# All products with the high weight parts before all with the low parts, within each output tile

## The chip, the cores and the metric

The kernel runs on one core of a Trainium2 chip. TensorE (PE) multiplies; ScalarE (ACT) and VectorE (DVE) prepare its operands and read its results; GpSimd (POOL) does some of the elementwise work; SyncE (SP) issues the loads of the weights. The metric is the device time of one execution in microseconds (us). Before the change it is 2869.92 us, the median of three runs (2869.36 to 2870.63).

## The reference, cut to what matters

The program is a two-layer trunk over 256 tokens with 2048 features. Each layer has a mixer, a cross attention to 256 memory tokens and a gated MLP of width 5632, each behind an RMS norm and each added to the running state `h`. The mixer of layer 0 is a short convolution beside a diagonal state-space scan ("S5"), that of layer 1 a sliding-window attention.

```python
def conv_ssm_mixer(h, w_in, ...):
    z = h @ w_in
    gate_b, gate_c, xa, u = jnp.split(z, [A_WIDTH, 2 * A_WIDTH, 3 * A_WIDTH], axis=-1)
    ya = gate_b * causal_dwconv(gate_c * xa, conv_w)
    ys = s5_branch(u, ...)
    return jnp.concatenate([ya, ys], axis=-1) @ w_out

def conv_gated_mlp(h, w_gate, w_up, conv_w, conv_b, w_down):
    g = causal_dwconv(h @ w_gate, conv_w) + conv_b
    return (jax.nn.silu(g) * (h @ w_up)) @ w_down
```

All of this is float32. Nearly all the arithmetic lies in the dense projections, `h @ w` with 128-feature blocks of both sides.

## The kernel before, in words

**Split operands.** Every weight block and every activation block is split into two parts, high and low, each in the reduced float32 format that TensorE takes (`fp32r`). Of the four products three are summed: high weight x high activation, high weight x low activation, low weight x high activation. An activation block is one tile `op`, 128x512: the high parts of 256 tokens, then the low parts of the same tokens.

**Output tiles.** A projection is computed in tiles of 128 output features (n-tiles), each a sum over K blocks of 128 input features (k-tiles; K is 16, or 11 in the MLP's down projection). `gemm` walks over the n-tiles. For each, `wload` has SP load one raw weight block, then ACT casts a chunk of 1024 columns (8 k-tiles) to its high part (`hi`, L90) and DVE subtracts to get the low part (`lo`, L91). A tile of 16 k-tiles has two chunks, which are called chunk 0 and chunk 1 here. The pools hold three raw blocks, four `hi` chunks and four `lo` chunks, so two n-tiles' worth of each: a chunk of n-tile i+2 is written into the place of the same chunk of n-tile i, once TensorE has read that for the last time.

**The matmuls.** `mm` takes the k-tiles in order. For each it issues one matmul of 512 columns with `hi` (L106, both activation parts, into the two halves of a PSUM bank) and one of 256 columns with `lo` (L107, into the first half), so that the two widths alternate. With `one` set (memory keys, gates, the very last tile) the 512-column matmul is replaced by two of 256 columns with the same `hi` (L103, L104). Each matmul loads its own 128x128 weights (PEld in the profile). The memory values (L326 to L328) and the attention values (L681 to L683) have the weights as the streamed operand and three matmuls per k-tile.

**Order of the work.** A scheduler orders the instructions of each engine when the program is built, by its own estimates; each engine then works through its list in order. So an ACT or DVE instruction that waits holds up all that stand behind it on its engine. TensorE's order is nearly that in which the code issues the matmuls.

**The stages.** Up to about 560 us the profile shows the even mixer: the first projection tiles (up to about 50 us), the memory keys (L103, L104, L107) and values (L326 to L328) of both layers, and the gates (from about 460 us, again L103, L104 and L107). Beside these DVE and ACT work through the S5 scan (L493 on ACT, L497 to L500 on DVE). The scan is handed out in portions, one behind each n-tile (`after`). Then follow the output projection, cross attention 0 (from about 720 us), MLP 0 (926 to 1653 us), the odd mixer (to about 1900 us), cross attention 1, and MLP 1 (2108 to 2837 us). In the odd mixer and in cross attention `half` puts a piece of the attention into the middle of an n-tile (in the odd mixer the transposes L745 of a head pair) and `after` puts other pieces behind it (the scores L713 and L716, then the values L759).

## Time and profile before

| what | value |
|---|---|
| median of three runs | 2869.92 us |
| span of the profiled execution | 2856.4 us |
| what the runs have beyond that span | 13.5 us |
| TensorE matmuls, busy | 2813.3 us, 98% of the span |
| VectorE busy | 1942.5 us, 68% |
| ScalarE busy | 1560.2 us, 55% |
| HBM read | 521.25 MB, 186 GB/s over the span |

The profile gives for the profiled execution its span, from the first to the last instruction; no other time of that execution is given. A busy share of TensorE counts overlapping matmuls as busy, so the pace of the matmuls is read from the start of one to the start of the next.

### The profile page before, as it was taken

Reading aid. Unit: us, or ns where it says so; the run is one execution under the profiler, and the core shown is the slowest. Engines: PE = TensorE matmul, PEld = TensorE weight load, DVE = VectorE, ACT = ScalarE, POOL = GpSimd, SP = SyncE. Lnnn points to the kernel's source line nnn. Section 1 sums busy time; section 2 is a strip of 40 time slices with the busy share of each in tenths; the row PEclk is TensorE's granted clock in tenths of the full one; section 3 lists DMA queues with packets and bytes.
Section 4 is the critical chain, followed back from the end, with each engine's and each line's share of the span. In section 5 each row is a group of like instructions: output and inputs, shape, how many; then the busy total and the mean of one; then the engine's idle time right before and its main releaser. Section 6 shows DMA issues by size and latency. Waiting matters only on the chain.

```text
span 2856.4 us, 44117 instructions
## 1 busy us (share of the span) xinstructions
PE 2813.3 (98%) x17163; PEld 2473.4 (87%) x17163; DVE 1942.5 (68%) x3130; ACT 1560.2 (55%) x2556; POOL 496.5 (17%) x484
## 2 busy tenths in 40 slices
PE   9999999999999999999999999999999999999998
PEld 8878978998988888888888888889888888888887
DVE  8978688757667666666666778776766566665655
ACT  7666766655554544545545567555555454454454
POOL 4100201322002320202202210110122022021121
PEclk9999999999999999999999999999999999999999
DMA  7455554545555556555455554464455554554544
GB/s 276 175 201 187 200 199 177 196 177 192 192 184 181 192 172 211 187 176 201 171 209 187 182 190 169 152 217 171 170 191 185 170 205 164 205 190 163 207 169 141
DMA packets 91811, 534.65 MB, mean 187 GB/s; under 512 B 10865, under 2 KB 17361, under 8 KB 40913
## 3 DMA queue, kind: packets, MB, share of 16 engines
q1 hardware_dynamic: 86368, 522.56, 51.8%
q10 hardware_dynamic: 5232, 9.26, 0.9%
q8 instruction: 134, 2.20, 0.3%
q14 instruction: 77, 0.62, 0.1%
HBM read 521.25 MB, written 10.53 MB: 186 GB/s over the span
## 4 chain that ended last, share of the span: by engine, by line
PE 90%; DVE 6%; ACT 3%; issue 1%; DMA 0%; POOL 0%; SPq 0%; DVEq 0%; ACTq 0%; POOLq 0%
PE ps L106 49%; PE ps L107 27%; PE ps L103 3%; PE ps L104 3%; DVE lo L91 2%; ACT stmp L493 2%; PE ps L327 1%; PE ps L326 1%; PE ps L328 1%; DVE stmp L497 1%; DVE S L498 1%; ACT hi L90 1%; PE m L850 1%; PE m L759 0%; DVE S L499 0%
## 5 line engine op out<-in xcount | busy, mean ns | idle before, releaser
L106 PE MATMUL ps<-op,hi 128*128 128x512 f32 x6069 | 2133.0, 397 | 0.7 <-DVE op L75 0.7
L107 PE MATMUL ps<-op,lo 128*128 128x256 f32 x6976 | 1956.3, 280 | 14.8 <-DVE lo L91 14.5
L91 DVE TENSOR_TENSOR lo<-raw,hi 128x1024 fp32r<-128x1024 f32 (+2 forms) x1033 | 1185.7, 1150 | 710.1 <-ACT hi L90 697.1
L90 ACT CAST hi<-raw 128x1024 fp32r<-128x1024 f32 (+2 forms) x1033 | 1009.9, 982 | 989.6 <-PE ps L106 822.6
L106 PEld LDWEIGHTS ps<-op,hi 128*128 128x128 f32 x6069 | 1138.9, 188 | 273.7 <-issue 3.0
L107 PEld LDWEIGHTS ps<-op,lo 128*128 128x128 f32 x6976 | 1319.1, 189 | 20.1 <-DVE lo L91 19.4
L103 PE MATMUL ps<-op,hi 128*128 128x256 f32 x907 | 259.1, 286 | 3.2 <-ACT hi L90 3.2
L104 PE MATMUL ps<-op,hi 128*128 128x256 f32 x907 | 257.7, 284 | 0.0
L167 POOL TENSOR_TENSOR acc<-acc,t 128x256 f32<-128x256 f32 x112 | 124.1, 1108 | 633.8 <-ACT t L169 627.3
L887 POOL TENSOR_TENSOR t<-t,rbc 128x256 f32<-128x256 f32 x88 | 71.4, 811 | 783.5 <-DVE t L156 752.2
L103 PEld LDWEIGHTS ps<-op,hi 128*128 128x128 f32 x907 | 175.0, 193 | 5.2 <-ACT hi L90 3.5
L104 PEld LDWEIGHTS ps<-op,hi 128*128 128x128 f32 x907 | 175.0, 193 | 0.1
L893 POOL TENSOR_TENSOR t<-t,rbc 128x256 f32<-128x256 f32 x88 | 124.2, 1411 | 289.2 <-ACT t L892 289.2
L493 ACT ACTIVATE stmp<-S,s_pw 128x256 f32<-128x256 f32 (+3 forms) x256 | 115.5, 526 | 41.2 <-DVE S L500 34.8
L327 PE MATMUL ps<-lo,op 128*128 128x512 f32 x256 | 101.6, 397 | 6.2 <-DVE lo L91 6.0
L326 PE MATMUL ps<-hi,op 128*128 128x512 f32 x256 | 101.3, 396 | 1.0 <-ACT hi L90 1.0
L328 PE MATMUL ps<-hi,op 128*128 128x512 f32 x256 | 100.5, 393 | 0.0
L156 DVE TENSOR_TENSOR t<-ps,t 128x256 f32<-128x256 f32 x232 | 96.5, 417 | 0.0
L68 DVE SCALAR_TENSOR_TENSOR op<-h,gains,op 128x256 fp32r<-128x256 f32 x96 | 83.6, 880 | 12.5 <-ACT op L67 12.5
L155 ACT COPY t<-ps 128x256 f32<-128x256 f32 x232 | 83.4, 361 | 3.0 <-PE ps L107 2.2
L305 POOL TENSOR_TENSOR kst<-t,rbc 128x256 f32<-128x256 f32 x32 | 32.7, 1022 | 261.3 <-DMA kv<-kst 131.6
L280 DVE TENSOR_TENSOR h<-h,ps 128x256 f32<-128x256 f32 x95 | 39.6, 419 | 50.9 <-PE ps L107 50.6
(218 smaller groups left out, 1858.9 us busy)
## 6 DMA issues: line engine op xcount, KB each, us to landing
raw<-in_ff_gate SPq DMA_DIRECT2D x88, 1024.0 KB, 4.8
raw<-in_ff_up SPq DMA_DIRECT2D x88, 1024.0 KB, 4.8
raw<-in_ff_down SPq DMA_DIRECT2D x128, 704.0 KB, 4.1
raw<-in_xa_k SPq DMA_DIRECT2D x32, 1024.0 KB, 4.9
raw<-in_xa_v SPq DMA_DIRECT2D x32, 1024.0 KB, 4.9
raw<-in_xa_q SPq DMA_DIRECT2D x32, 1024.0 KB, 4.8
raw<-in_xa_o SPq DMA_DIRECT2D x32, 1024.0 KB, 4.8
raw<-in_ev_w_in SPq DMA_DIRECT2D x28, 1024.0 KB, 4.9
```

The costliest lines, as they stand in the source:

```text
L90: nc.scalar.copy(hi, s)
L91: nc.vector.tensor_tensor(lo, s, hi.bitcast(F32), op=ALU.subtract)
L103: nc.tensor.matmul(ps[:, :T], lhsT=hi, rhs=o[:, :T], start=k == 0, stop=False)
L104: nc.tensor.matmul(ps[:, :T], lhsT=hi, rhs=o[:, T:], start=False, stop=False)
L106: nc.tensor.matmul(ps, lhsT=hi, rhs=o, start=k == 0, stop=False)
L107: nc.tensor.matmul(ps[:, :T], lhsT=lo, rhs=o[:, :T], start=False, stop=k == K - 1)
L167: nc.gpsimd.tensor_tensor(self.acc, self.acc, self.sq, op=ALU.add)
L326: nc.tensor.matmul(ps[b], lhsT=xh, rhs=hi, start=k == 0, stop=False)
L327: nc.tensor.matmul(ps[b], lhsT=xh, rhs=lo, start=False, stop=False)
L328: nc.tensor.matmul(ps[b], lhsT=xl, rhs=hi, start=False, stop=k == KT - 1)
L493: nc.scalar.activation(tmp[:, x, :, p - p0, :], at(0, both, p), AF.Copy, scale=pw[:, x, k, 8 * b + p:8 * b + p + 1])
L893: nc.gpsimd.tensor_tensor(y, y, self.rbc, op=ALU.mult)
```

## The change

Within each n-tile the matmuls with `hi` of all k-tiles now come first, then those with `lo` of all k-tiles. `mm` is divided into `mm_hi` and `mm_lo`. `half` is called between the two phases, where it was called after half of the k-tiles. The first four n-tiles of the input projection do the same within each loaded step of 1 to 4 k-tiles, and the memory values and the attention values within each loaded weight block. The number and shape of all instructions stay as they were. The rest of the diff takes comments away and moves lines.

```diff
-    def mm(self, ps, w, ops, k0, k1, K, one=False):
+    def mm_hi(self, ps, w, ops, k0, k1, one=False):
         nc = self.nc
         for k in range(k0, k1):
-            hi, lo = w[k]
-            o = ops[k]
+            hi, o = w[k][0], ops[k]
             if one:
                 nc.tensor.matmul(ps[:, :T], lhsT=hi, rhs=o[:, :T], start=k == 0, stop=False)
                 nc.tensor.matmul(ps[:, :T], lhsT=hi, rhs=o[:, T:], start=False, stop=False)
             else:
                 nc.tensor.matmul(ps, lhsT=hi, rhs=o, start=k == 0, stop=False)
-            nc.tensor.matmul(ps[:, :T], lhsT=lo, rhs=o[:, :T], start=False, stop=k == K - 1)
+
+    def mm_lo(self, ps, w, ops, k0, k1, K):
+
+        for k in range(k0, k1):
+            self.nc.tensor.matmul(ps[:, :T], lhsT=w[k][1], rhs=ops[k][:, :T], start=False, stop=k == K - 1)
+
+    def mm(self, ps, w, ops, k0, k1, K, one=False, half=None):
+
+        self.mm_hi(ps, w, ops, k0, k1, one)
+        if half is not None:
+            half()
+        self.mm_lo(ps, w, ops, k0, k1, K)
...
-            if half is None:
-                self.mm(ps, w, ops, 0, k1, K, one(n) if callable(one) else one)
-            else:
-                self.mm(ps, w, ops, 0, K // 2, K, one)
-                half(n)
-                self.mm(ps, w, ops, K // 2, k1, K, one)
+            self.mm(ps, w, ops, 0, k1, K, one(n) if callable(one) else one, half=None if half is None else lambda: half(n))
...
-                        nc.tensor.matmul(ps[b], lhsT=xh, rhs=hi, start=k == 0, stop=False)
-                        nc.tensor.matmul(ps[b], lhsT=xh, rhs=lo, start=False, stop=False)
-                        nc.tensor.matmul(ps[b], lhsT=xl, rhs=hi, start=False, stop=k == KT - 1)
+                        nc.tensor.matmul(ps[b], lhsT=o[:, b * P:(b + 1) * P], rhs=w[j][0], start=k == 0, stop=False)
+                        nc.tensor.matmul(ps[b], lhsT=o[:, T + b * P:T + (b + 1) * P], rhs=w[j][0], start=False, stop=False)
+                for j in range(4):
+                    k = 4 * q + j
+                    for b in range(2):
+                        nc.tensor.matmul(ps[b], lhsT=self.memop[k][:, b * P:(b + 1) * P], rhs=w[j][1], start=False, stop=k == KT - 1)
```

Two places show what the scheduler makes of it. The first is TensorE in the odd mixer, inside the n-tile whose sum is `ps_18707` (K is 16; `hi_18699` and `lo_18700` are its chunk 0, `hi_18703` and `lo_18704` its chunk 1, `s_18600` or `s_18597` the weights of a head pair that are transposed). Before:

```order
L107 MATMUL ps_18707<-op_17933,lo_18700 128x256
L106 MATMUL ps_18707<-op_18035,hi_18699 128x512
L107 MATMUL ps_18707<-op_18035,lo_18700 128x256
L745 MATMUL m_18724<-ident_91,s_18600 128x128 x3
L745 MATMUL m_18730<-ident_91,s_18600 128x128 x3
L106 MATMUL ps_18707<-op_18137,hi_18703 128x512
L107 MATMUL ps_18707<-op_18137,lo_18704 128x256
L106 MATMUL ps_18707<-op_18239,hi_18703 128x512
L107 MATMUL ps_18707<-op_18239,lo_18704 128x256
L106 MATMUL ps_18707<-op_18341,hi_18703 128x512
```

And now:

```order
L105 MATMUL ps_18707<-op_18341,hi_18703 128x512
L105 MATMUL ps_18707<-op_18443,hi_18703 128x512
L105 MATMUL ps_18707<-op_18545,hi_18703 128x512
L751 MATMUL m_18721<-ident_91,s_18597 128x128 x3
L751 MATMUL m_18727<-ident_91,s_18597 128x128 x3
L110 MATMUL ps_18707<-op_17321,lo_18700 128x256
L110 MATMUL ps_18707<-op_17423,lo_18700 128x256
L110 MATMUL ps_18707<-op_17525,lo_18700 128x256
```

The transposes stood between the 8th and the 9th k-tile, with matmuls of both widths on either side. Now all 16 wide matmuls are in front of them and all 16 narrow ones behind.

The second is DVE in the memory keys of layer 0, where it makes the low parts for the n-tile with raw block `raw_1707` among steps of the scan (`S_966` is the state, `stmp` its temporaries). Before:

```order
L498 TENSOR_TENSOR S_966<-S_966,stmp_2193 128x512
L91 TENSOR_TENSOR lo_1710<-raw_1707,hi_1709 128x1024
L499 TENSOR_TENSOR S_966<-S_966,stmp_2193 128x256
L500 TENSOR_TENSOR S_966<-S_966,stmp_2193 128x256
L497 TENSOR_TENSOR stmp_2315<-S_966,s5_pw_1391 128x256 x2
L498 TENSOR_TENSOR S_966<-S_966,stmp_2315 128x256
L91 TENSOR_TENSOR lo_1714<-raw_1707,hi_1713 128x1024
L499 TENSOR_TENSOR S_966<-S_966,stmp_2315 128x128
L500 TENSOR_TENSOR S_966<-S_966,stmp_2315 128x128
L497 TENSOR_TENSOR stmp_2387<-S_966,s5_pw_1391 128x128 x2
```

And now:

```order
L502 TENSOR_TENSOR stmp_2193<-S_966,s5_pw_1391 128x512 x2
L503 TENSOR_TENSOR S_966<-S_966,stmp_2193 128x512
L504 TENSOR_TENSOR S_966<-S_966,stmp_2193 128x256
L91 TENSOR_TENSOR lo_1710<-raw_1707,hi_1709 128x1024
L91 TENSOR_TENSOR lo_1714<-raw_1707,hi_1713 128x1024
L505 TENSOR_TENSOR S_966<-S_966,stmp_2193 128x256
L502 TENSOR_TENSOR stmp_2315<-S_966,s5_pw_1391 128x256 x2
L503 TENSOR_TENSOR S_966<-S_966,stmp_2315 128x256
L504 TENSOR_TENSOR S_966<-S_966,stmp_2315 128x128
```

The scan steps that stood between the low parts of chunk 0 and chunk 1 have moved out of that gap: the two low parts of an n-tile now stand next to each other.

The third is DVE in the odd mixer, between one head pair (`s_17388`, with its softmax numbers `st_17399`) and the next (`s_17490`, which reads the scores in `m_17491`). Before:

```order
L732 TENSOR_TENSOR st_17399<-st_17399 128x4
L733 RECIPROCAL st_17399<-st_17399 128x4
L736 TENSOR_SCALAR s_17388<-s_17388,st_17399 128x256
L736 TENSOR_SCALAR s_17388<-s_17388,st_17399 128x128
L736 TENSOR_SCALAR s_17388<-s_17388,st_17399 128x256
L736 TENSOR_SCALAR s_17388<-s_17388,st_17399 128x128
L91 TENSOR_TENSOR lo_17637<-raw_17630,hi_17636 128x1024
L156 TENSOR_TENSOR t_17481<-ps_17436,t_17482 128x256
L718 SCALAR_TENSOR_TENSOR s_17490<-m_17491,bias_17488 128x256
L719 SCALAR_TENSOR_TENSOR s_17490<-m_17491,bias_17488 128x128
```

And now:

```order
L91 TENSOR_TENSOR lo_17633<-raw_17630,hi_17632 128x1024
L91 TENSOR_TENSOR lo_17637<-raw_17630,hi_17636 128x1024
L738 TENSOR_TENSOR st_17399<-st_17399 128x4
L161 TENSOR_TENSOR t_17481<-ps_17436,t_17482 128x256
L739 RECIPROCAL st_17399<-st_17399 128x4
L724 SCALAR_TENSOR_TENSOR s_17490<-m_17491,bias_17488 128x256
L742 TENSOR_SCALAR s_17388<-s_17388,st_17399 128x256
L742 TENSOR_SCALAR s_17388<-s_17388,st_17399 128x128
L742 TENSOR_SCALAR s_17388<-s_17388,st_17399 128x256
L742 TENSOR_SCALAR s_17388<-s_17388,st_17399 128x128
L725 SCALAR_TENSOR_TENSOR s_17490<-m_17491,bias_17488 128x128
```

Before, the low part of chunk 0 of the n-tile with raw block `raw_17630` stood ahead of the reciprocal (it is not among these rows), that of chunk 1 between the scaling of one head pair and the reading of the next scores. Now both stand ahead of the reciprocal, and the scaling follows the first reading of the next scores.

## Rows read from the trace of the kernel before

**Rows 1.** The page: the span, and of the chain of work that ended last the shares by engine.

```profile
span 2856.4 us, 44117 instructions
...
PE 90%; DVE 6%; ACT 3%; issue 1%; DMA 0%; POOL 0%; SPq 0%; DVEq 0%; ACTq 0%; POOLq 0%
```

**Rows 2.** What TensorE waited for, by stretch: first 0 to 35 us (two rows), then 110 to 166, 166 to 355 (two rows), 355 to 400 (two rows) and 475 to 530 us (two rows). Columns: engine, tile and line that waited, what released it; us in total, times, longest us.

```profile
PE ps L254 <- DVE lo L91: 2.1, 4, 0.9
PE ps L253 <- ACT hi L90: 1.8, 2, 1.5
...
PE ps L107 <- DVE lo L91: 9.3, 10, 1.7
...
PE ps L327 <- DVE lo L91: 1.9, 3, 1.1
PE ps L107 <- DVE lo L91: 0.7, 2, 0.5
...
PE ps L327 <- DVE lo L91: 4.2, 6, 1.4
PE ps L326 <- ACT hi L90: 1.0, 1, 1.0
...
PE ps L107 <- DVE lo L91: 4.2, 4, 1.3
PE ps L103 <- ACT hi L90: 3.2, 1, 3.2
```

**Rows 3.** Stretches of the trace, of the 512-column matmuls L106 alone: start and end, length, PE busy (x matmuls), PEld busy (x loads), granted clock, DMA share, GB/s. In each stretch the widths alternate, so the count is one of pairs.

```profile
626.00:706.00 80.00, 80.00 (x227) 42.54 (x227) 1.00 0.52 186
926.00:1653.00 727.00, 726.80 (x2097) 392.85 (x2097) 1.00 0.55 190
1670.00:1900.00 230.00, 193.38 (x537) 100.73 (x537) 1.00 0.48 168
2108.00:2837.00 729.00, 728.80 (x2063) 387.46 (x2063) 1.00 0.52 183
```

**Rows 4.** The timeline of TensorE where matmuls of one width follow each other: start us, us, line, shapes. Between the first two rows lie 35 further matmuls of 256 columns (so 36 steps), between the next two 18 of 512 columns (19 steps), between the last two 11 of 256 columns (12 steps), each with its own weight load.

```profile
99.75 0.28 PE L103 MATMUL ps<-op,hi 128*128 128x256 f32 x1
...
104.07 0.28 PE L103 MATMUL ps<-op,hi 128*128 128x256 f32 x1
...
420.00 0.39 PE L327 MATMUL ps<-lo,op 128*128 128x512 f32 x1
...
424.31 0.39 PE L328 MATMUL ps<-hi,op 128*128 128x512 f32 x1
...
2840.06 0.28 PE L107 MATMUL ps<-op,lo 128*128 128x256 f32 x1
...
2841.50 0.29 PE L107 MATMUL ps<-op,lo 128*128 128x256 f32 x1
```

**Rows 5.** The same timeline behind a stop of TensorE in the memory values, all of 512 columns: 9 steps from the first row to the second, 4 from the second to the third.

```profile
425.87 0.39 PE L327 MATMUL ps<-lo,op 128*128 128x512 f32 x1
...
427.95 0.39 PE L327 MATMUL ps<-lo,op 128*128 128x512 f32 x1
...
428.86 0.39 PE L328 MATMUL ps<-hi,op 128*128 128x512 f32 x1
```

**Rows 6.** Stretches with all engines: start and end, length, busy us (x instructions) of PE, PEld, DVE, ACT, POOL, then granted clock, DMA share, GB/s.

```profile
116.00:155.00 39.00, 30.50 (x237) 28.68 (x237) 36.95 (x71) 16.05 (x26) 3.72 (x5) 1.00 0.43 156
...
355.00:400.00 45.00, 39.65 (x193) 30.00 (x193) 41.22 (x84) 23.56 (x39) 3.13 (x2) 0.96 0.44 160
...
460.00:520.00 60.00, 52.48 (x426) 49.69 (x426) 53.95 (x95) 32.86 (x59) 12.22 (x11) 0.97 0.48 171
```

**Rows 7.** The timeline of TensorE at a wait for a low part (the first two rows), at the wait for a high part (the next two), and from there on: 24 steps lie between the last two rows. In brackets the idle time before and what ended it.

```profile
122.74 0.28 PE L104 MATMUL ps<-op,hi 128*128 128x256 f32 x1
124.76 0.39 PE L107 MATMUL ps<-op,lo 128*128 128x256 f32 x1 [1.74 <-DVE lo L91]
...
512.81 0.28 PE L107 MATMUL ps<-op,lo 128*128 128x256 f32 x1
516.25 0.39 PE L103 MATMUL ps<-op,hi 128*128 128x256 f32 x1 [3.16 <-ACT hi L90]
...
517.88 0.41 PE L103 MATMUL ps<-op,hi 128*128 128x256 f32 x1
...
523.00 0.41 PE L103 MATMUL ps<-op,hi 128*128 128x256 f32 x1
```

**Rows 8.** A short stretch of TensorE right behind that wait: start and end, length, PE busy (x), granted clock, DMA share, GB/s.

```profile
517.00:520.00 3.00, 2.49 (x11) 0.50 0.29 116
```

**Rows 9.** The timeline of ACT before that wait: a step of the scan and the cast for which TensorE waited.

```profile
504.34 3.02 ACT L493 ACTIVATE stmp<-S,s_pw 128x126 f32<-128x126 f32 x7 [9.83 <-DVE S L500]
...
515.15 1.04 ACT L90 CAST hi<-raw 128x1024 fp32r<-128x1024 f32 x1
```

**Rows 10.** The timeline of one n-tile's end in the odd mixer: DVE makes a low part, ACT copies a head pair's transposed weights (`pT`), TensorE runs scores (L713) and values (L759).

```profile
1734.13 1.22 DVE L91 TENSOR_TENSOR lo<-raw,hi 128x1024 fp32r<-128x1024 f32 x1
1736.09 0.83 ACT L748 COPY pT<-m 128x384 f32<-128x384 f32 x2
1736.25 0.70 PE L713 MATMUL m<-kT,q 64*128 64x256 f32 x4
1737.10 0.88 PE L759 MATMUL m<-pT,vt 128*64 128x128 f32 x12
```

More of the change, by code (lines that the diff above doesn't have):

```diff
@@ L138, in gemm @@
         for n, w, ps in held:
-            self.mm(ps, w, ops, K - late, K, K, one)
+            self.mm(ps, w, ops, K - late, K, K, one(n) if callable(one) else one)
             if mid2 is None:
@@ L677, in odd_mixer @@
                     k = 8 * q + j
[L678 removed]
                     for b in range(2):
[L680 to L683 removed]
+                        nc.tensor.matmul(pv[b][:, :T], lhsT=xs[k][:, b * P:(b + 1) * P], rhs=w[j][0], start=k == 0, stop=False)
+                        nc.tensor.matmul(pv[b][:, :T], lhsT=xs[k][:, T + b * P:T + (b + 1) * P], rhs=w[j][0], start=False, stop=False)
+                for j in range(8):
+                    k = 8 * q + j
+                    for b in range(2):
+                        nc.tensor.matmul(pv[b][:, :T], lhsT=xs[k][:, b * P:(b + 1) * P], rhs=w[j][1], start=False, stop=k == KT - 1)
                 if q == 0:
```

24 lines of the change are left out of this document (8 added, 16 removed).

## The prediction

> **What bounds the kernel now.** The page comes first: the chain of work that ended last is 90% TensorE in a span of 2856.4 us [rows 1]. So TensorE's list of matmuls is the path, and only two things can change the time: the pace at which matmuls follow each other, and the time TensorE stands still. The number and shape of the matmuls stay as they are.
>
> The second view is what TensorE waited for, by stretch [rows 2]. Behind the start-up it waits only up to 530 us, beside the S5 scan, for DVE's low parts (9.3 + 1.9 + 0.7 + 4.2 + 4.2 = 20.3 us in 25 waits) and for ACT's high parts (1.0 + 3.2 = 4.2 us in 2). DVE is nearly full there: 36.95 of 39 us, 41.22 of 45, 53.95 of 60 [rows 6].
>
> The third view is the pace, from starts of matmuls. Where the widths alternate, a pair (512 then 256 columns) takes 727.00 / 2097 = 0.3467 us in MLP 0, but 729.00 / 2063 = 0.3534 us in MLP 1, and 80.00 / 227 = 0.3524 us in the even mixer's output projection, all at granted clock 1.00 with TensorE busy throughout [rows 3]. The same pair has two paces, 6.7 ns apart, and nothing that waits explains it. The fourth view is runs of one width: 256 columns take (104.07 - 99.75) / 36 = 0.1200 us, and again (2841.50 - 2840.06) / 12 = 0.1200 us in the very last tile, right behind the slow MLP 1; 512 columns take (424.31 - 420.00) / 19 = 0.2268 us [rows 4]. A pair made of such steps costs 0.2268 + 0.1200 = 0.3468 us, the faster of the two paces.
>
> **The change part by part.**
>
> *Pace.* Inside a phase every matmul now follows one of its own width. I price a pair at 0.3468 us everywhere. MLP 1 gains 2063 x (0.3534 - 0.3468) = 13.6 us; the output projection of the even mixer, 16 n-tiles of 16 pairs, 256 x (0.3524 - 0.3468) = 1.4 us; the odd mixer, with 537 pairs [rows 3], 537 x 0.0066 = 3.5 us if they run at MLP 1's pace. That last pace is an assumption, since its row mixes in the attention's small matmuls. MLP 0 loses 2097 x 0.0001 = 0.2 us. Sum: 18 us less. The two changes of width per n-tile I price at nothing, because alternation is nothing but changes of width and its faster pace equals the sum of the pure ones. What no row shows is 512 columns directly behind 256 with no stop, followed by more 512. The nearest row is the memory values behind a stop: nine steps at (427.95 - 425.87) / 9 = 0.2311 us before they settle at 0.2275 [rows 5]. By it each n-tile would pay 9 x (0.2311 - 0.2268) = 0.04 us; over 422 n-tiles with wide matmuls (counted from the code) that is 16 us. I take zero, and keep -18 and -2 as the ends.
>
> The Trainium skill ("TensorE: Matmul & The Clock Gate", section "Back-to-back issue gap") gives the isolated gap between matmuls as set by the column count alone, about N/2.4 + 2.5 ns when the clock is up. By that rule a pair is an estimated 325 ns in any order, and reordering is worth nothing. The trace disagrees with both halves: the pair takes 0.3467 us or 0.3534 us, not one value. That order has no effect on the pace is a rival below, priced from rows.
>
> *Low parts are wanted later.* In the memory keys and gates an n-tile is 48 steps of 0.12 us, 5.76 us. Before, `lo` of chunk 0 was wanted at the third matmul (0.24 us in) and `lo` of chunk 1 at 3.1 us; now at 32 x 0.12 = 3.84 us and 4.80 us. DVE's order has the two low parts side by side, that of chunk 0 behind about the same scan steps as before, that of chunk 1 behind fewer. So a DVE that runs late may be 3.6 us later before TensorE notices. That is a stock that is spent once in each stretch where DVE is the slower engine, not a gain per tile: DVE's work is unchanged and it has only 2 of 39 us free. Keys, 110 to 166 us: 3.6 of 9.3 us. From 166 to 355 us: five separate waits, none over 1.1 us, all inside the stock: 2.6 us, and 5 x 0.16 us for starting again (124.76 - 122.74, less 1.74 idle and one step of 0.12 [rows 7]), 3.4 us. Memory values, 355 to 400 us: a block's low parts are wanted 16 wide steps later instead of one, 15 x 0.2268 = 3.4 us of the 4.2 + 0.2. Gates, 475 to 530 us: 3.6 of 4.2 us. Sum: 14 us less. The ends are 0 (the scheduler has moved scan work in front and eats the stock) and all 20.3 + 4.2 us of waits with 27 x 0.16 us of restarts and the clock loss behind the longest, 24 steps at (523.00 - 517.88) / 24 = 0.2133 instead of 0.12 us, 2.2 us, at a granted clock of 0.50 [rows 7, 8]: 31 us.
>
> *High parts.* `hi` of chunk 0 is wanted at the start of its tile, as before, and that of chunk 1 a third into it instead of half: 0.96 us earlier in the keys and gates. Each `hi` buffer also comes free earlier, a third and two thirds into its last tile instead of half and the end. Outside the scan TensorE waits for no cast at all, so I price this at 0 there. Inside the scan ACT may stand behind a scan step that waits for DVE, as it did for 9.83 us before the cast that ended at 516.19 [rows 9]. I leave that wait of 3.2 us where it is. DVE's wait for a free `lo` buffer moves from half a tile to five sixths; what stands behind it on DVE (scan steps, evacuations) has four PSUM banks of slack.
>
> *`half` between the phases.* In the odd mixer the transposes now stand 16 x 0.12 = 1.9 us before the tile's end instead of 8 x 0.3534 = 2.8 us. ACT's copy of their result is the margin: it ends at 1736.92 and the values start at 1737.10, 0.18 us later, behind the scores at 1736.25 [rows 10]. The copy started over 2 us after its transposes because the softmax stands before it on ACT, and DVE's low part of 1.22 us is one of the things that softmax competes with. Pairing the low parts can bring that chain forward or push it by one low part. The ends: 0, and 13 tiles x (1.22 - 0.18) = 13.5 us. I take 0: both low parts now stand ahead of the reciprocal on DVE, where the second can start when its buffer comes free at the tile's end, so they are about done when the next scores come, and none is left between the scaling and the reading of those scores.
>
> *Start and end.* The first 35 us have 3.9 us of waits [rows 2]; phases of up to 16 wide matmuls tolerate a late low part but want four operands at once. I take 0, with 2 us either way. Behind the last matmul nothing changes.
>
> **Sum.** -18 - 14 = -32 us on the profiled span of 2856.4 us, which gives 2824 us. The runs have 13.5 us beyond that span, which no instruction of the change touches: 2869.9 - 32 = 2838 us.
>
> **The rivals.**
>
> *A. Order does not set the pace*: the 6.7 ns of MLP 1 come from something that outlasts the reorder, such as the addresses of the operands. For it: that pace holds evenly over 729 us. Against it: the last tile runs at 0.1200 us right behind. The 18 us are gone: 2856 us.
>
> *B. Wide matmuls settle anew in each tile* [rows 5]. The 16 us come back: 2854 us. Against it: rows 5 follow a stop, and the phases follow none.
>
> *C. The stock is eaten*: DVE is full beside the scan, and its waits return at their old length. 2852 us.
>
> *D. Slower.* The casts become the bound beside the scan. A third instead of half a tile takes 0.96 us from every cast of chunk 1; in ACT's list it stands behind scan steps that wait for DVE [rows 9]. If it is late in each of the 27 places where TensorE waits today, that is 26 us; the old waits stay, and the odd mixer loses its 13.5 us: 2870 - 18 + 26 + 13 = 2891 us, or 2878 us without the odd mixer. It decides where casts end less than 0.96 us before use. Against it: ACT is half idle there, 16.05 of 39 us busy [rows 6].
>
> **How the numbers follow.** The forecast has 0.56, with a range of its own of 2824 to 2850 us; A 0.13, B 0.11, C 0.12, D 0.08. About 0.2% (5.7 us, so 2864 to 2876 us) is what a measurement of this kernel can tell from no change. The forecast, C and nearly all of A and B are faster: 0.85; two rivals that meet, as A with C, come to 2870 us, and I give 0.08 to no change; slower has D's remainder, 0.07. The range is 2822 us (all the pace and nearly twice the stock) to 2864 us (A with most of C).
>
> **What would show it.** Pace right: 512-column steps of 0.227 us and 256-column steps of 0.120 us in both MLPs, and MLP 1 as long as MLP 0. A: MLP 1 stays at 0.353 us per pair. B: the first nine wide steps of each tile near 0.231 us. Stock right: waits for low parts up to 530 us fall from 20 us to about 8 us. C: they keep their sum. D: waits for ACT's casts grow from 4 us to tens of us, or TensorE waits for `pT` in the odd mixer. The forecast is wrong if MLP 0 becomes longer than 727 us, or if any wait of TensorE appears behind 530 us.

## The result and the profile after

The changed kernel takes 2851.07 us, the median of 4 runs (2850.46 to 2852.47). Beside it the kernel before takes 2869.68 us (4 runs, 2869.36 to 2870.63). The ratio is 0.9936, with a 95% interval of 0.9921 to 0.9951: faster by 0.64%, 18.6 us. The forecast was 2838 us with a range of 2822 to 2864 us. The sign and the range hold; the centre is 13 us too low.

The profiled execution after has a span of 2849.5 us and a time of 2851.28 us, 1.8 us more. The profiled execution before had a span of 2856.4 us [rows 1]. The two spans therefore differ by 6.9 us only, not by 18.6 us, and that is the first thing to explain.

The page after, span and chain, as in [rows 1]:

```profile
span 2849.5 us, 44158 instructions
...
PE 90%; DVE 4%; ACT 3%; issue 1%; DMA 1%; POOL 1%; SPq 0%; DVEq 0%; ACTq 0%; POOLq 0%
```

TensorE is still the path. The program cuts itself into stages at the small matmuls that sum the statistics (m<-ones,acc, L181 before and L186 after). Their starts give this account of the two profiled executions, in us:

| stage | before | after | difference |
|---|---|---|---|
| start and even mixer | 719.00 | 715.18 | -3.8 |
| cross attention 0 | 204.85 | 203.20 | -1.7 |
| MLP 0 | 733.06 | 736.94 | +3.9 |
| odd mixer | 245.01 | 249.05 | +4.0 |
| cross attention 1 | 203.12 | 203.20 | +0.1 |
| MLP 1 | 736.58 | 726.60 | -10.0 |
| the rest | 14.8 | 15.3 | +0.5 |

MLP 1 got faster, as forecast, but MLP 0 and the odd mixer got slower, and the even mixer gained 4 us where 15 were expected. The first row needs a caution. Six kernels of the experiments (q4, pair2, best, best2, half_early, u_odd) have the same instruction lists up to 700 us as the changed kernel, and in their profiled executions the even mixer ends at 715.9, 716.5, 716.7, 717.7, 718.3 and 720.7 us. In b_again and m0, which have the lists of the kernel before up to there, it ends at 719.8 and 718.3 us. So two executions of the same lists can differ by up to 5.5 us in this stage. With the two kernels' own ends, the mean is 717.3 us with phases and 719.0 us without: on average the stage gained nearer 2 us than 4.

Most of what TensorE waited for after (columns as in [rows 2]):

```profile
PE ps L102 <- ACT hi L90: 9.6, 10, 2.8
PE m L210 <- DVE t L208: 8.1, 3, 3.6
PE ps L328 <- ACT hi L90: 5.9, 5, 3.5
PE ps L110 <- DVE lo L91: 3.8, 3, 1.7
PE ps L105 <- DVE op L75: 1.8, 3, 0.7
...
PE ps L333 <- DVE lo L91: 1.1, 1, 1.1
```

Waits for low parts (L110, L333) are 4.9 us, where [rows 2] had 20.3 us beside the scan and 2.1 us at the start. Beside the scan the waits for ACT's high parts went from 4.2 to 15.5 us (L102, L328). Two lines grew: DVE t L208, the broadcast of the statistics, which TensorE met only once before, at the very end (2.7 us), and DVE op L75, operands that TensorE wants as soon as they are made, as in the down projections (0.7 us in one wait before).

The pace in MLP 1, from TensorE's timeline after; the last three rows look at a phase from inside (start us, us, line, count from there on, in windows of their own):

```profile
2198.23 3.82 PE L105 MATMUL ps<-op,hi 128*128 128x512 f32 x16
2201.88 2.08 PE L110 MATMUL ps<-op,lo 128*128 128x256 f32 x16
2203.79 3.82 PE L105 MATMUL ps<-op,hi 128*128 128x512 f32 x16
...
2203.79 0.40 PE L105 MATMUL ps<-op,hi 128*128 128x512 f32 x1
2204.72 0.85 PE L105 MATMUL ps<-op,hi 128*128 128x512 f32 x3
2206.99 0.62 PE L105 MATMUL ps<-op,hi 128*128 128x512 f32 x2
```

An n-tile of 16 pairs lasts 2203.79 - 2198.23 = 5.56 us, 0.3475 us per pair. The first four wide steps behind narrow ones take (2204.72 - 2203.79) / 4 = 0.2325 us each, the ten from the fifth on (2206.99 - 2204.72) / 10 = 0.2270 us. Over all n-tiles of the MLP the records give 233.3, 235.8, 228.3, 232.4 and 230.8 ns for the first five wide steps, then 226.7 ns; 113.3 and 119.2 ns for the first two narrow ones, then 120.0 ns. The sum is 19.6 ns more per n-tile than settled steps would take: rival B exists, at half its size.

### The profile page after: what moved, and what is told of

Its sections match the earlier page's. It is cut to its first block, busy times and chain, and to the rows that moved or that the text cites. A ratio compares the mean times of both kernels' runs of the same rounds, so it can differ in the third digit from the quotient of the medians.

```text
span 2849.5 us, 44158 instructions
## 1 busy us (share of the span) xinstructions
PE 2806.3 (98%) x17163; PEld 2491.4 (87%) x17163; DVE 1963.9 (69%) x3130; ACT 1573.2 (55%) x2556; POOL 457.9 (16%) x484
## 4 chain that ended last, share of the span: by engine, by line
PE 90%; DVE 4%; ACT 3%; issue 1%; DMA 1%; POOL 1%; SPq 0%; DVEq 0%; ACTq 0%; POOLq 0%
PE ps L105 48%; PE ps L110 28%; PE ps L102 2%; PE ps L103 2%; PE ps L328 2%; PE ps L329 2%; PE ps L333 2%; DVE lo L91 1%; ACT stmp L498 1%; ACT hi L90 1%; PE m L856 1%; PE m L765 1%; DVE stmp L502 1%; DMA kv<-kst 1%; DVE S L503 0%
## 5 line engine op out<-in xcount | busy, mean ns | idle before, releaser
L91 DVE TENSOR_TENSOR lo<-raw,hi 128x1024 fp32r<-128x1024 f32 (+2 forms) x1033 | 1207.8, 1192 | 405.5 <-ACT hi L90 175.2
L105 PE MATMUL ps<-op,hi 128*128 128x512 f32 x6069 | 1463.3, 391 | 2.6 <-DVE op L75 1.8
L105 PEld LDWEIGHTS ps<-op,hi 128*128 128x128 f32 x6069 | 1111.8, 188 | 220.9 <-issue 3.2
L110 PEld LDWEIGHTS ps<-op,lo 128*128 128x128 f32 x6976 | 897.6, 191 | 37.1 <-DVE lo L91 4.9
L110 PE MATMUL ps<-op,lo 128*128 128x256 f32 x6976 | 918.4, 283 | 3.9 <-DVE lo L91 3.8
L102 PE MATMUL ps<-op,hi 128*128 128x256 f32 x907 | 224.3, 287 | 9.7 <-ACT hi L90 9.6
L103 PE MATMUL ps<-op,hi 128*128 128x256 f32 x907 | 221.7, 284 | 0.0
L172 POOL TENSOR_TENSOR acc<-acc,t 128x256 f32<-128x256 f32 x112 | 105.2, 939 | 654.7 <-ACT t L174 649.7
L102 PEld LDWEIGHTS ps<-op,hi 128*128 128x128 f32 x907 | 174.9, 193 | 14.3 <-ACT hi L90 12.5
L103 PEld LDWEIGHTS ps<-op,hi 128*128 128x128 f32 x907 | 175.1, 193 | 0.1
L896 DVE SCALAR_TENSOR_TENSOR t<-t,ff_conv 128x255 f32<-128x255 f32 x88 | 42.9, 488 | 141.7 <-ACT t L895 141.7
L75 DVE TENSOR_TENSOR op<-t,op 128x256 fp32r<-128x256 f32 x104 | 43.8, 425 | 124.5 <-ACT op L74 124.3
L328 PE MATMUL ps<-hi,op 128*128 128x512 f32 x256 | 102.1, 399 | 6.0 <-ACT hi L90 5.9
L905 POOL TENSOR_TENSOR t<-t 128x256 f32<-128x256 f32 x88 | 67.2, 764 | 135.0 <-DVE t L161 134.7
```

The costliest lines, as they stand in the source:

```text
L91: nc.vector.tensor_tensor(lo, s, hi.bitcast(F32), op=ALU.subtract)
L102: nc.tensor.matmul(ps[:, :T], lhsT=hi, rhs=o[:, :T], start=k == 0, stop=False)
L103: nc.tensor.matmul(ps[:, :T], lhsT=hi, rhs=o[:, T:], start=False, stop=False)
L105: nc.tensor.matmul(ps, lhsT=hi, rhs=o, start=k == 0, stop=False)
L110: self.nc.tensor.matmul(ps[:, :T], lhsT=w[k][1], rhs=ops[k][:, :T], start=False, stop=k == K - 1)
L172: nc.gpsimd.tensor_tensor(self.acc, self.acc, self.sq, op=ALU.add)
```

## The experiments

The kernel before ran once more, and eleven further kernels. Each time is set beside runs of the kernel before on the same chip; their medians were 2869.0 us (b_again, u_s5, u_odd, pair2), 2868.9 us (m0, half_early, deep, best) and 2869.7 us (q4, best2, thin_b, thin_a). The changed kernel itself was not timed again beside them. With the even mixer varying as said above, 2 or 3 us between its 2851.07 us and the median of a later kernel tell little. The lengths of the later stages tell more: in the kernels with phases they repeat to 0.2 us where a stage was not edited.

### Which kernel before is being compared? (b_again, m0)

The kernel before, once more, for its time beside its span:

> The kernel before, unchanged, profiled once more. The changed kernel's executions have a span 1.8 us below their time, so the 13.5 us between the span of before that was shown and the timed median look too large to lie outside the instructions. Theory P (alternating widths have more than one steady pace, and an execution can take either in MLP 0): the span is about 2868 us, 1.8 below the time of about 2870, and MLP 0 runs at 0.353 us per pair where the earlier profile has 0.347; that is 2100 x 0.0066 = 13.9 us. Rival Q (the 13.5 us lie outside the span of this kernel): span about 2856 us again, time about 2870, MLP 0 at 0.347.

It took 2859.09 us at a span of 2857.3 us: 1.8 us lie outside. So the "13.5 us beyond the span" do not exist; the profiled execution is a faster one than most of the timed ones. Its MLP 0 again alternated at 346.7 ns per pair and its MLP 1 at 353.3 ns. The 37 runs of the kernel before that were timed in this study fall into groups:

```
32 runs   2866.6 to 2871.8 us
 4 runs   2855.7 to 2858.4 us
 1 run    2843.8 us
```

The steps between the groups are about 13 us, and one MLP at the slow instead of the fast pace is 2112 pairs (88 n-tiles of 16, 64 of 11) x 6.6 ns = 13.9 us. This suggests that most runs have both MLPs slow, the profiled ones one, and a single run none. All three profiled executions in which MLP 0 alternates (before, b_again and, for most of the MLP, thin_b) had it fast; whether the profiling has a part in that, no run shows. No profile of a run with both slow was taken, so m0 tests it: the kernel before with phases in MLP 0 alone.

```diff
-            if half is None:
+            if half is None and self.ph:
+                self.mm_ph(ps, w, ops, 0, k1, K)
+            elif half is None:
...
+            self.ph = l == 0
             xs = self.mlp(l, xs, G_MIX + 1 if l == 0 else None)
+            self.ph = False
```

> The kernel before with the phases in MLP 0 alone; all else alternates. It tells which pace MLP 0 had in the timed runs of the kernel before. Theory 1 (two paces: in the profiled executions, 2858 to 2859 us, MLP 0 takes the fast alternation and MLP 1 the slow one, in the timed ones, 2869 us, both take the slow one): MLP 0 alternating slowly would last 733.1 us and 2071 x 6.6 ns = 746.8 us, with phases it lasts 736.9 us as in the changed kernel; the median falls by 10 us, to 2859 to 2860 us. Theory 2 (the forecast's: MLP 0 is fast in the timed runs as in the profile, and the rest of the median lies outside the span): the median rises by 3.9 us, to 2873 us. In the profiled execution both expect MLP 0 at 737 us and, where MLP 1 keeps its slow pace of 353.3 ns per pair, a span of 2860 us.

Measured: 2860.29 us (six runs, 2846.47 to 2861.55), ratio 0.9966 (0.9944 to 0.9988). That is what theory 1 expected: replacing MLP 0, which in the profile makes it longer by 4 us, shortens the timed run by 8.6 us. The profiled execution of m0 took 2860.33 us, so here profile and median agree. The one run of 2846.47 us lies 13.8 us below the median, as a run should in which MLP 1, too, is fast. In m0's profile MLP 0 lasts 737.1 us and MLP 1 alternates as in the last of [rows 3], 729 us for 2063 pairs:

```profile
2108.00:2837.00 729.00, 728.80 (x2063) 387.44 (x2062) 1.00 0.52 184
```

So the timed gain of 18.6 us is the 6.9 us between the profiles plus about 12 us, nearly the price of the slow pace in MLP 0, which by m0 was slow where the time was taken and fast where the profile was taken.

### What a change of width costs (q4, pair2)

q4 divides the n-tiles of the MLPs into shorter phases (`ph` is 4):

```diff
+                for k in range(0, K, ph):
+                    self.mm_hi(ps, w, ops, k, min(k + ph, K))
+                    self.mm_lo(ps, w, ops, k, min(k + ph, K), K)
```

> The changed kernel with phases of four k-tiles in both MLPs (four wide, four narrow, and so on) instead of one pair of phases per n-tile. Theory W (each return from narrow to wide matmuls costs anew, as the first five wide steps behind narrow ones take 233.3, 235.8, 228.3, 232.4 and 230.8 ns instead of 226.7, and two narrow ones save 7.5 ns): four wide and four narrow cost 15.5 ns more than their settled steps; an n-tile of 16 pays 62 instead of 20 ns, one of 11 some 41 instead of 20 ns; 86 x 42 + 64 x 21 = 5 us per MLP: MLP 1 rises from 726.6 to 731.6 us, MLP 0 from 736.9 to 741.9 us, the time to 2861 us. Theory T (the price belongs to the start of an n-tile, with its new bank and new weights): both MLPs stay, 2851 us.

Measured: 2861.53 us (7 runs, 2859.85 to 2863.12), 10 us above the changed kernel; in the profile MLP 0 lasts 740.8 us and MLP 1 730.5 us, 3.9 us more each, so 7.8 of the 10 us. Theory W names the mechanism; its 5 us per MLP were a little too many. Its timeline (from the start of one block in MLP 1 to the start of the next but one):

```profile
2202.53 1.09 PE L105 MATMUL ps<-op,hi 128*128 128x512 f32 x4
2203.45 0.64 PE L110 MATMUL ps<-op,lo 128*128 128x256 f32 x4
...
2205.33 1.09 PE L105 MATMUL ps<-op,hi 128*128 128x512 f32 x4
```

One block lies between. A block of four pairs lasts (2205.33 - 2202.53) / 2 = 1.40 us, 0.350 us per pair: between the two paces of alternation. The price is one of the return to wide matmuls, not of the n-tile.

pair2 goes the other way: high parts of two n-tiles, then low parts of both, half the returns.

```diff
+            for j in range(2):
+                self.mm_hi(pss[j], ws[j], ops, 0, K, ones[j])
+            for j in range(2):
+                self.mm_lo(pss[j], ws[j], ops, 0, K, K)
+                finish(n_tiles[i + j], pss[j])
```

> The changed kernel with longer phases in the two MLPs: high parts of two n-tiles, then low parts of both, so half as many changes of width. In the changed kernel the first five wide steps of each n-tile are 27 ns longer in sum than the settled 226.7 ns and the first two narrow ones 7 ns shorter: 20 ns per n-tile. Theory B (the price hangs on the change of width): 304 n-tiles x 10 ns = 3 us less, 2848 us, with 20 ns per pair of n-tiles in place of 40. Rival (the price hangs on the n-tile, as a new PSUM bank or a new weight chunk): 2851, and the second n-tile of a phase pays its 27 ns again.

Measured: 2856.08 us (6 runs, 2854.55 to 2858.70). Both theories missed: it is slower than the changed kernel by 5 us. In the profile MLP 0 is 0.4 us and MLP 1 2.7 us longer, so not all of the 5 us is accounted for. Two n-tiles now take 11.11 us instead of 11.13 us, so the settling did halve, but before the last slab's down projection TensorE stood still for its operands. The timeline there, and the granted clock just behind (stretch, length, PE busy, clock):

```profile
2778.26 1.43 PE L105 MATMUL ps<-op,hi 128*128 128x512 f32 x5 [1.99 <-DVE op L75]
```

```profile
2779.50:2782.50 3.00, 3.00 (x16) 0.54 0.02 5
```

16 narrow matmuls behind the wait need 3 us instead of 1.9 us, at a granted clock of 0.54, near the lower of the engine's two levels, 1.2 GHz. The wait is the line DVE op L75, grown from 0.5 us in the changed kernel to 2.0 us: a phase of 11 wide matmuls reads its eleven operands in 2.5 us, alternation in 3.8 us, and pairing also evacuates the last two tiles ahead of it together.

### Beside the scan (u_s5, deep, thin_b, thin_a)

The forecast counted on 14 us of fewer waits. The question is whether the waits belong to the order or to a shortage of weights that no order can cure. u_s5 puts alternation back in the memory keys, the memory values and the gates:

```diff
+            if one is True:
+                self.mm_alt(ps, w, ops, 0, k1, K, True)
+            else:
+                self.mm(ps, w, ops, 0, k1, K, one(n) if callable(one) else one, half=None if half is None else lambda: half(n))
...
+                        nc.tensor.matmul(ps[b], lhsT=o[:, b * P:(b + 1) * P], rhs=w[j][1], start=False, stop=False)
```

> The changed kernel with the memory keys, the memory values and the gates put back to alternation; all else in phases. Measured so far: the part up to the output projection of the even mixer is only about 3.8 us shorter than before, and TensorE's waits there have moved from low parts (20.3 to 4.9 us) to high parts (4.2 to 14 us). Theory C (the stock is eaten: DVE is the bound beside the scan, the order only changes for what TensorE waits): 2851 + 2 to 4 = 2853 to 2855 us, waits for low parts back near 20 us. Rival (the stock as predicted, 14 us, but hidden by something else that grew): 2860 to 2865 us.

Measured: 2856.38 us (7 runs, 2854.80 to 2857.59), 5 us above the changed kernel, which ran at another time. On the chip of u_s5 there ran u_odd and pair2, which have the changed kernel's lists up to 700 us. Behind the even mixer their profiles are 6.0 us shorter and 2.2 us longer than the changed kernel's; taking that out of their times gives 2853.8 and 2853.9 us for the changed kernel on this chip (an estimate), and u_s5, 0.5 us shorter there, comes to 2856.8 us. So the phases are worth about 3 us in these places, as theory C gave and far less than 14. TensorE waits 18.3 us for low parts again and 4.2 us for high parts. In deep ACT has a fifth buffer for high parts during the scan:

```diff
+            if self.hx is not None and self.nhi % 5 == 0:
+                hi = self.hx.tile([P, m * n], F32R, name="hi", tag="hi")
...
-                B = pool.tile([P, 2, 2, P], F32R, name="BT", tag="BT", bufs=2)
+                B = pool.tile([P, 2, 2, P], F32R, name="BT", tag="BT", bufs=1)
```

> The changed kernel with a fifth buffer for high parts while the scan runs (one small scan buffer goes from two copies to one to make room). In the changed kernel TensorE waits about 15 us for ACT's high parts beside the scan and about 5 us for low parts, in place of 4 and 20 us. Theory H (the high parts are wanted earlier in each n-tile, and their four buffers hold too little ahead): the fifth buffer takes most of the 15 us, the even mixer falls from 647 to 635 to 640 us, the time to 2840 to 2845 us. Theory C (ACT and DVE together bring weights, with the scan between them, more slowly than TensorE takes them, and the place of the wait is all that the order decides): the waits keep their sum within 4 us, the time stays at 2847 to 2853 us.

Measured: 2849.60 us (4 runs, 2846.69 to 2851.48), as theory C expected. TensorE's waits between 110 and 560 us:

```profile
PE ps L114 <- DVE lo L95: 13.9, 13, 2.1
PE ps L106 <- ACT hi L94: 2.6, 5, 1.2
PE ps L332 <- ACT hi L94: 1.9, 2, 1.2
PE ps L337 <- DVE lo L95: 1.3, 2, 1.1
```

The high parts are now nearly always in time, 4.5 us, and the waits moved back to the low parts, 15.2 us: 19.7 us in all against 20.4 us in the changed kernel (18.0 to 24.4 us in the six further executions of its lists). Last, two of the three additions of each scan step are left out, in both orders:

```diff
-                    v.tensor_tensor(at(m, 0, pa), at(m, 0, pa), tmp[:, 1, 1], op=ALU.subtract)
-                    v.tensor_tensor(at(m, 1, pa), at(m, 1, pa), tmp[:, 1, 0], op=ALU.add)
```

> The kernel before with two of the three additions of each scan step left out (the output is not the reference's): DVE loses about 80 of its 353 us between 110 and 560 us. Theory C (beside the scan the weights come more slowly than TensorE takes them, and the order only decides which cast it waits for): with the shortage gone the waits for casts between 110 and 560 us fall from 24 us to under 6 us. Theory O (the waits belong to the order, each order has its own late casts): they fall by less than half.

> The changed kernel with the same two additions left out. Theory C: waits for casts between 110 and 560 us fall from 20 us to under 6 us, and the even mixer ends within 2 us of the other order's, less what the pace of its output projection gives (1.4 us). Theory O (phases want the high parts in a burst at the head of each n-tile, which ACT can't give): 8 us or more of waits for ACT's high parts stay, and the even mixer is longer than with alternation.

thin_b took 2852.90 us and thin_a 2836.84 us, one run each. The same waits, 110 to 560 us, of thin_b:

```profile
PE ps L107 <- DVE lo L91: 11.4, 15, 1.8
PE ps L327 <- DVE lo L91: 6.4, 9, 1.2
PE ps L103 <- ACT hi L90: 3.7, 3, 2.5
```

and of thin_a:

```profile
PE ps L102 <- ACT hi L90: 5.4, 5, 3.6
PE ps L328 <- ACT hi L90: 1.2, 2, 0.7
PE ps L110 <- DVE lo L91: 1.1, 1, 1.1
PE ps L333 <- DVE lo L91: 0.7, 1, 0.7
```

Neither theory holds alone. With alternation 21.5 of 24.5 us stay although DVE lost a sixth of its work (353 to 296 us busy): theory O is right for the old order, where a low part is wanted one or two matmuls behind its high part, so that (as I read it; no run moves these steps alone) any scan step that stands between the two casts shows. With phases 8.4 us of waits are left, 1.8 us of them for low parts, where thin_b has 21.5 and 17.8 us: there theory C is nearly right, except that it expected the two orders to end within 2 us of each other: the even mixer ends 11.9 us earlier than with alternation (700.49 against 712.40 us), more than executions of one list differ by. So with a lighter scan the phases save 13.1 us of waits, close to the 14 us that the prediction booked. In the full kernel the scan eats that stock: behind the old waits stood a shortage of nearly the same size.

### The odd mixer (u_odd, half_early)

After the change an n-tile of the q projection ends like this. First TensorE's timeline, then ACT's (casts, the start of the softmax L734, the copies) and the DVE step L733 that the softmax needs, then the waits of the weight loads over the whole odd mixer:

```profile
1729.72 3.95 PE L105 MATMUL ps<-op,hi 128*128 128x512 f32 x16
1733.51 0.81 PE L751 MATMUL m<-ident,s 128*128 128x128 f32 x6
1734.08 2.16 PE L110 MATMUL ps<-op,lo 128*128 128x256 f32 x16
1736.16 0.70 PE L719 MATMUL m<-kT,q 64*128 64x256 f32 x4
...
1737.08 1.24 PE L765 MATMUL m<-pT,vt 128*64 128x128 f32 x12
1738.25 0.96 PE L105 MATMUL ps<-op,hi 128*128 128x512 f32 x3
```

```profile
1733.76 1.05 ACT L90 CAST hi<-raw 128x1024 fp32r<-128x1024 f32 x1 [0.79 <-PE ps L105]
1734.72 0.20 ACT L734 ACTIVATE st<-st 128x4 f32<-128x4 f32 x1
...
1736.58 0.82 ACT L754 COPY pT<-m 128x384 f32<-128x384 f32 x2
...
1733.57 0.16 DVE L733 TENSOR_TENSOR st<-st,sinks 128x4 f32<-128x4 f32 x1
```

```profile
PEld m L765 <- ACT pT L754: 4.7, 25, 0.3
```

The values need both copies that ACT runs from 1736.58 on. The n-tile lasts 1738.25 - 1729.72 = 8.53 us, and the values 1.24 us where [rows 10] had 0.88. The margin of 0.18 us is gone. The transposes now come 1.9 instead of 2.8 us before the tile's end, but they are done at 1734.32, and the copies start 2.3 us later, because the softmax stands before them on ACT. The same places in the kernel before, in the n-tile of [rows 10]:

```profile
1732.85 1.05 ACT L90 CAST hi<-raw 128x1024 fp32r<-128x1024 f32 x1
1734.22 0.21 ACT L728 ACTIVATE st<-st 128x4 f32<-128x4 f32 x1 [0.32 <-DVE st L727]
...
1734.02 0.16 DVE L727 TENSOR_TENSOR st<-st,sinks 128x4 f32<-128x4 f32 x1
```

There ACT waited for DVE's step, which ended at 1734.18, and began the softmax at 1734.22. Now that step ends at 1733.73, but the softmax begins only at 1734.72: in front of it on ACT stands the n-tile's second cast, which waited for TensorE to finish the wide phase, and which stood behind the copies before (at 1736.82). By this reading the cast delays the copies by about 1.0 us in this n-tile; no run moves that cast alone. u_odd puts alternation, and the transposes in its middle, back into this projection alone:

```diff
+            if alt:
+                self.mm_alt(ps, w, ops, 0, K // 2, K)
+                half(n)
+                self.mm_alt(ps, w, ops, K // 2, k1, K)
```

> The changed kernel with the query projection of the odd mixer put back: alternation, and the transposes in the middle of the n-tile. Measured so far: the odd mixer is 4.0 us longer than before, and the values wait for ACT's copy of the transposed weights in each n-tile. Theory M (the margin of 0.18 us is gone because the transposes stand 0.9 us nearer to the values): these waits vanish, 13 tiles x about 0.4 us: 2851 - 5 = 2846 us. Rival S (the loss is the settling of the wide matmuls behind each of the small attention pieces, so it stays whatever the place of the transposes, or alternation pays as much in its slow pace): within 1 us of 2851.

Measured: 2847.76 us (4 runs, 2847.02 to 2850.80), ratio 0.9932 (0.9910 to 0.9954). In the profile the odd mixer falls from 249.05 to 243.57 us, below the 245.01 us of before; the span (2849.0 us) hardly falls, as the even mixer of that execution ends 5.5 us later with the same lists. ACT's order is the old one again: cast, softmax, copies, cast. So the loss lies in this projection's order, as theory M expected, but the run does not tell the place of the transposes from the cast. half_early keeps the phases and moves the transposes into the middle of the wide phase:

```diff
+                self.mm_hi(ps, w, ops, 0, K // 2)
+                half(n)
+                self.mm_hi(ps, w, ops, K // 2, K)
+                self.mm_lo(ps, w, ops, 0, K, K)
```

> The changed kernel, with the transposes of the odd mixer's q projection moved from between the phases to the middle of the wide phase: 8 wide matmuls earlier, 1.8 us. The phases stay. Theory W (the odd mixer grew from 245.0 to 249.1 us because the values now wait for ACT's copy of the transposes, 0.19 and 0.18 us in each of 13 n-tiles): those waits go, the n-tile falls from 8.53 to about 8.15 us, the stage to about 244 us, the time from 2851.1 to 2846 us. Theory S (it grew because the phases settle anew behind each break): one more break adds at most 27 ns per n-tile, the stage stays at 249 to 250 us and the time at 2851 to 2852 us.

Measured: 2850.28 us (4 runs, 2849.59 to 2852.34); the odd mixer lasts 246.9 us, between the two theories. Its weight loads wait:

```profile
PEld m L757 <- DVE s L731: 2.6, 10, 0.5
...
PEld m L757 <- ACT pT L760: 0.4, 1, 0.4
```

The values' wait for pT went, and the transposes themselves now wait for the softmax that DVE scales (s, L731). But the scheduler also put the copies (at 1735.42 us) ahead of the next softmax (1736.15) on ACT, so this run, too, moves more than the transposes. Between the softmax and the values there is hardly any slack; the old place, in the middle of an alternating tile, served both ends.

### Towards a better version (best, best2)

best joins u_odd with pairs of n-tiles in the MLPs, except in the last slab's down projection, whose first n-tile alternates:

> The changed kernel with alternation back in the odd mixer's q projection (2847.8 us alone), with the MLPs' n-tiles taken two by two (high parts of both, low parts of both) except in the last slab's down projection, and with the first n-tile of that projection alternating. Theory A (settling is paid once per return to wide matmuls, 20 ns, and the earlier pairing lost time only by waits of the last slab): pairing saves about 1.2 us per MLP, the waits for operands at the last slab (0.7 us each) go, 2843 to 2845 us. Theory B (pairing itself costs elsewhere, as two evacuations come at once): 2849 to 2853 us.

Measured: 2849.29 us (4 runs, 2847.38 to 2849.73), theory B, and no faster than u_odd alone. The timeline again showed waits of 2.1 us for DVE op L75 in each MLP, from the gate and up tiles of the last operand, which were paired and so evacuated together. best2 leaves these two unpaired:

```diff
-        while two and i + 1 < len(n_tiles):
+        while two and i + 1 < len(n_tiles) - (2 if two == 2 else 0):
```

> The version of the last batch (2849.3 us), in which the waits for operands before the last slab's down projection (2.1 us in each MLP) came from the pairing of the gate and up tiles just ahead of it: those two tiles are no longer paired. Theory A: the waits go to under 0.5 us each, the MLPs last 735 and 724.7 us, the time is 2844 to 2846 us. Theory B (the pairing costs elsewhere): 2848 to 2850 us.

Measured: 2845.19 us (4 runs, 2843.45 to 2845.89), ratio 0.9913 (0.9899 to 0.9928), the fastest version here with the whole scan. The time is theory A's. The MLPs gained less than that theory gave (736.0 and 725.7 us), and the waits fell from 2.1 to 0.8 us in each MLP, not under 0.5.

## Why the prediction was right or wrong

**"The runs have 13.5 us beyond that span, which no instruction of the change touches"** is the step that failed first. 1.8 us lie beyond the span. The rest is MLP 0 at the slow pace in the timed runs, as m0 shows by its time (no profile has caught it). The sum on the profiled span, 2824 us, was 25 us too low against 2849.5 us: of the 32 us that were booked, 6.9 came. The final 2838 us is only 13 us off because the timed runs gained about 9 us in MLP 0 (8.6 in m0) where the prediction booked a loss of 0.2. To that extent the total is right by luck. The cause, a slow pace of alternation that the phases take away, is the prediction's own, but it placed it in MLP 1 alone.

**Pace, MLP 1: -13.6 us.** Right in mechanism, over-sized. Measured -10.0 us: the settling, 152 n-tiles (88 of 16 k-tiles, 64 of 11) x 19.6 ns = 3.0 us, and 0.6 us of the wait for operands were left out (13.6 - 3.0 - 0.6 = 10.0). "The two changes of width per n-tile I price at nothing" is the term that was mis-sized: they cost 19.6 ns per n-tile. The other end that was kept, 40 ns, was twice too high, and the middle would have been right.

**Pace, MLP 0: +0.2 us.** In the profile +3.9 us, by the same settling and the same wait. Both signs that were named for being wrong appeared: an MLP 0 longer than before, and waits of TensorE behind 530 us (DVE op L75). The second sign was no test, as the kernel before already had two such waits, 0.7 us for DVE op L75 and 2.7 us at the very end: "it waits only up to 530 us" was misread. In the timed runs the sign turns, by m0.

**Pace elsewhere.** Cross attention 0 gained 1.7 us that were not priced; its output projection had also alternated at 353 ns per pair. That, too, differs between executions: m0, which alternates there as well, took the fast pace and lasted 203.2 us, as long as with phases.

**Stock of later low parts: -14 us.** The low-part waits fell further than forecast, from 20.3 to 4.9 us. But "I leave that wait of 3.2 us where it is", said of ACT, was wrong: the high-part waits grew to 15.5 us. Between 110 and 560 us the sum of waits fell by 24.5 - 20.4 = 4.1 us, and in the six further executions of the changed kernel's lists it is 18.0 to 24.4 us. That is rival C, through the other cast.

**Start: 0, 2 us either way.** The waits for casts at the start fell from 3.9 to 1.5 us (in the six further executions they are 1.7 to 3.8 us), but a stop behind it was missed. TensorE in the changed kernel, and DVE there:

```profile
68.04 0.50 PE L186 MATMUL m<-ones,acc 128*128 128x1 f32 x4
...
78.02 1.22 PE L210 MATMUL m<-t,ones 128*128 128x256 f32 x2 [3.62 <-DVE t L208]
```

```profile
72.33 1.23 DVE L91 TENSOR_TENSOR lo<-raw,hi 128x1024 fp32r<-128x1024 f32 x1
73.47 0.15 DVE L190 TENSOR_SCALAR v<-m 128x2 f32<-128x2 f32 x1
73.54 1.22 DVE L91 TENSOR_TENSOR lo<-raw,hi 128x1024 fp32r<-128x1024 f32 x1
```

and in the kernel before:

```profile
69.15 0.28 PE L181 MATMUL m<-ones,acc 128*128 128x1 f32 x2
```

```profile
70.77 0.15 DVE L185 TENSOR_SCALAR v<-m 128x2 f32<-128x2 f32 x1
```

DVE reads the sums (v<-m) 5.4 us behind the matmul instead of 1.6 us: the scheduler now places it between two low parts. TensorE stands still for 3.62 us and then runs at a granted clock of 0.54, near its lower level of 1.2 GHz, for a while:

```profile
78.50:85.00 6.50, 6.50 (x45) 0.54 0.54 180
```

The same statistics cost 1.83 us at 43.8 us. Taking from every step between two starts of matmuls its settled length and adding up those that are over 0.12 us late, TensorE stood still for 1.5 us before and 8.8 us after between 35 and 110 us, and for 33.4 us before and 27.1 us after between 110 and 560 us (25.6 to 32.1 us in the six further executions). The first undoes what the phases gained in the second. No run took it away by itself; the other kernels with phases show the same two waits (4.2 to 5.0 us).

**Odd mixer: -3.5 us of pace and 0 for `half`.** Measured +4.0 us. "I take 0" is the step. The pairing of the low parts did bring DVE's side of the softmax forward: its last step ended 2.07 us before the next scores and now ends 2.43 us before them. But ACT's second cast moved in front of the softmax, and the thin margin was gone, with 1.24 - 0.88 = 0.36 us per n-tile; the end that was kept had 1.04 us. The prediction knew that each `hi` buffer comes free earlier, and priced it at 0 because TensorE waits for no cast outside the scan. A cast can also hold up what stands behind it in ACT's list. The rest of the mixer (values and output projection) did gain 1.4 us (u_odd against before).

**Rivals.** A fell: order sets the pace, in MLP 1 and in m0, though alternation can take the fast pace too, as in MLP 0 of the profile before. B is true at half its size. C is true in sum but not in kind. D is true in kind, with waits for ACT's casts 11 us longer instead of 26 and waits for pT of 5 us instead of 13, but the low-part waits that it left standing went, so it did not turn the sign.

## What to carry to other kernels

Time and profile may come from different executions: compare the profiled execution's own time with the timed median before any sum is made on the span, and if they differ look for a stage whose pace varies. Before a stage's few us are put down to an edit, see how much executions of the same instruction list differ there. Grouping matmuls of one width removes a pace that varies, at a price per change of width, so groups should be long, but each longer group wants all its operands earlier, and the first tile behind a dependency is where that is paid. Before a wait is booked as gain, ask which other producer would be late next: here the low parts' slack was real and was filled by the high parts, until the scan was made lighter. And when buffers come free earlier, ask what the earlier refill will now stand in front of on its own engine.

## What was not expected of the hardware

- An alternation of 512 and 256 columns has at least two repeating patterns on the same instructions at full granted clock: one at 346.7 ns per pair, one of three pairs that take 1060 ns (starts 117, 241, 120, 236, 113 and 233 ns apart). The pattern differs between executions: in the even mixer's output projection the kernel before was slow and m0, with the same instruction lists up to there, fast. In before, b_again and m0 a pattern, once taken, lasted through a whole MLP; in thin_b's MLP 0 the fast one turned into the slow one at 1582 us, with no wait in the profile. The counts of 512-column matmuls in 50 us at granted clock 1.00 show both (as in [rows 3]; 640 to 690 us of before, then of m0; 1590 to 1640 us of before, then of thin_b):

```profile
640.00:690.00 50.00, 50.00 (x143) 1.00 0.50 181
640.00:690.00 50.00, 50.00 (x145) 1.00 0.53 191
...
1590.00:1640.00 50.00, 50.00 (x146) 1.00 0.57 186
1590.00:1640.00 50.00, 50.00 (x143) 1.00 0.62 208
```

- The slow pattern loses 1060 - 3 x 346.7 = 20 ns per three pairs, the phases 19.6 ns per return to wide matmuls. Whether that is one and the same loss, and what chooses the pattern, stays open: no run forced either pattern.
- The Trainium skill ("TensorE: Matmul & The Clock Gate", section "Back-to-back issue gap") gives an isolated gap between matmuls that depends on the column count alone. The settled steps, 226.7 and 120.0 ns, would allow such a rule with another constant, but here the gap behind the same instruction depends on what ran before it (a 256-column step takes 113, 119 or 120 ns in a phase).
- With phases in both MLPs the 4 runs of the changed kernel lie within 2.0 us, where those of the kernel before spread over 28 us (2843.8 to 2871.8); no kernel with phases in both MLPs spreads over more than 4.8 us, and m0, with phases in one, spreads over 15 us. The fastest single run of before, 2843.77 us, is faster than any run of the changed kernel: the phases replace a pace that is usually slow, but not always, by a price that is paid in every run.
